# Branch products 2 and 1 of a hybrid decoder layer in seven block products instead of eight

## The chip, the cores and the metric

One core of one Trainium2 chip runs the whole kernel. The metric is the device time of one execution in microseconds (us), the median of three runs. TensorE is called PE, VectorE DVE, ScalarE ACT, GpSimd POOL and SyncE SP; SP issues most loads.

## The reference

All is float32. 576 tokens (512 of a prompt, 64 of eight samples) go through one layer; the two groups are stacked.

```python
xn = rmsnorm(x); proj = xn @ w_in                      # 1024 -> 13440 columns
y_conv = b_gate * conv3(c_gate * h) * silu(g_conv)     # branch 0
y_rwkv = rwkv7(p_shift, ...) * silu(g_rwkv)            # branch 1
y_mem  = attention(q_mem, mem_k, mem_v) * silu(g_mem)  # branch 2
merged = (sigmoid(m_conv) * (y_conv @ w_branch[0])
        + sigmoid(m_rwkv) * (y_rwkv @ w_branch[1])
        + sigmoid(m_mem)  * (y_mem  @ w_branch[2]))    # w_branch[i]: 1024 x 1024
y = rmsnorm(x + merged @ w_out)
```

Also returned are the memory keys and values and the new states.

## The kernel before

**Products.** Activations lie transposed, 128 features by 576 tokens, eight such tiles `k` for 1024 features. Each float32 operand is split into a high part (rounded to float32r) and a low part (the rest), and a product takes three matmuls: high by high, high by low, low by high. `mm` makes one output tile of 128 features: 8 tiles `k` x 3 terms x 2 halves of 288 tokens = 48 matmuls of 288 columns. Its weights are two loads of 128x512 (`wload`): ACT writes the high part `wh`, POOL subtracts for the low part `wl`; both have three buffers.

**The order of the work.** The order of PE's instructions is the order of the Python code. On the other engines a scheduler sets the order of the instructions when the kernel is built, and each engine then runs its list strictly in that order. The last stages run in this order:

1. `drive(gate(WGM, qt))`: eight products with `w_in`; each gives silu(g_mem) and is multiplied into one tile of `qt` (the attention's output).
2. `drive(branch(2, *split(qt)))`: `split` makes the parts `yh`, `yl`. For each output tile `j` there is the gate (a product with `w_in`, or a load if it was made early, in idle slots of the RWKV stage) and the product with `w_br`. DVE multiplies the gate `th` (tile `ev`) by the product in PSUM, POOL adds it to `acc`.
3. `drive(gate(WGR, ow))`: the same as 1 for the RWKV output (tiles `ts4`, `ts4b`).
4. `drive(branch(1, ...))`, where POOL's sum goes on to ACT (`mgh`, the high part) and DVE (`mgl`, the low part). `wout(0)` loads and splits half of `w_out` beside it.
5. The product with `w_out`, the residual and the last norm (L1284).

Seven gates were made early, those of branch 1 for `j` 0 to 6; the other nine are made in stages 2 and 4. PSUM tile `m` (`pm`) has two buffers of two banks. One line of a helper stands for many places: L93 is every `tensor_tensor`, L96 every `scalar_tensor_tensor`, L99 every activation, L245 the matmul in `mm`.

## Time and profile before

| what | us |
|---|---|
| median of 3 runs (1234.75 to 1237.21) | 1235.94 |
| the profiled execution | 1235.45 |
| its span in the trace | 1233.6 |
| PE busy in the span | 1186.9 |
| DVE busy in the span | 587.0 |
| ACT busy in the span | 524.9 |
| POOL busy in the span | 573.8 |

Busy times are unions over the whole span; 1.85 us of the profiled execution lie outside the span. A busy PE means that matmuls follow each other without a gap; it does not say how fast one is.

### The profile page before, as it was taken

The page shows a single profiled execution, that of the slowest core. Times are in us where ns is not written, and L with a number is a line of the kernel's source. Part 1 is how long each engine was busy: PE and PEld are TensorE (multiplying, and loading weights), DVE is VectorE, ACT ScalarE, POOL GpSimd, SP SyncE. Part 2 cuts the span into 40 slices and gives each one's busy share as a digit, 9 for nine tenths or more (in the row PEclk, how much of TensorE's full clock was granted, in tenths as well). Part 3 has the DMA queues.
Part 4 walks back from the last instruction along what each step waited for, and adds up shares of the span by engine and source line. Part 5 has one row for each costly group of instructions (what it writes and reads, how often), then busy time and mean ns, then how long its engine had stood idle before and what let it go on. Part 6 is the DMA issues. An engine that isn't in the chain of part 4 may idle for free. (4 is left out here: it accounts for less than half of the span.)

```text
span 1233.6 us, 25594 instructions
## 1 busy us (share of the span) xinstructions
PE 1186.9 (96%) x10158; PEld 1100.8 (89%) x10158; DVE 587.0 (48%) x1514; ACT 524.9 (43%) x1120; POOL 573.8 (47%) x521
## 2 busy tenths in 40 slices
PE   7999979999899999999989999999999999999997
PEld 7798979989798988988879898889899999999976
DVE  7856866468675686647673315213113100134233
ACT  6563446435463544546344435333233222233222
POOL 4535532555535465454543545333334454446642
PEclk9999989999999999999999999999999999999999
DMA  8642222132321322222322225653632222225522
GB/s 290 213 126 72 70 72 63 59 91 58 91 65 53 89 68 84 90 86 70 110 80 74 69 71 171 195 181 123 208 97 87 80 84 86 78 86 161 161 105 78
DMA packets 93056, 129.39 MB, mean 105 GB/s; under 512 B 36988, under 2 KB 41320, under 8 KB 92936
## 3 DMA queue, kind: packets, MB, share of 16 engines
q1 hardware_dynamic: 55888, 110.20, 28.3%
q10 hardware_dynamic: 37048, 17.56, 5.4%
q8 instruction: 80, 1.31, 0.5%
q14 instruction: 40, 0.33, 0.1%
HBM read 115.96 MB, written 11.47 MB: 103 GB/s over the span
## 5 line engine op out<-in xcount | busy, mean ns | idle before, releaser
L93 POOL TENSOR_TENSOR wl<-w,wh 128x512 fp32r<-128x512 f32 x274 | 366.5, 1340 | 490.0 <-ACT wh L99 451.4
L245 PE MATMUL m<-xh,wh 128*128 128x288 f32 x1680 | 370.4, 302 | 0.5 <-ACT vst L99 0.5
L245 PE MATMUL m<-xl,wh 128*128 128x288 f32 x1680 | 369.4, 301 | 0.0
L245 PE MATMUL m<-xh,wl 128*128 128x288 f32 x1680 | 365.2, 299 | 0.0
L99 ACT ACTIVATE wh<-w 128x512 fp32r<-128x512 f32 x290 | 180.5, 627 | 294.2 <-PE m L245 169.1
L245 PEld LDWEIGHTS m<-xh,wh 128*128 128x128 f32 x1680 | 268.8, 189 | 8.6 <-issue 3.7
L245 PEld LDWEIGHTS m<-xl,wh 128*128 128x128 f32 x1680 | 269.2, 189 | 6.4 <-issue 2.9
L245 PEld LDWEIGHTS m<-xh,wl 128*128 128x128 f32 x1680 | 269.4, 189 | 3.0 <-issue 2.1
L96 DVE SCALAR_TENSOR_TENSOR ev<-ev,m 128x576 f32<-128x576 f32 x32 | 24.2, 755 | 168.4 <-PE m L245 110.3
L245 PE MATMUL m<-yh,wh 128*128 128x288 f32 x384 | 82.9, 297 | 0.0
L245 PE MATMUL m<-yh,wl 128*128 128x288 f32 x384 | 82.8, 297 | 0.0
L245 PE MATMUL m<-yl,wh 128*128 128x288 f32 x384 | 82.8, 297 | 0.0
L245 PEld LDWEIGHTS m<-yh,wl 128*128 128x128 f32 x384 | 61.7, 188 | 2.1 <-issue 2.1
L245 PEld LDWEIGHTS m<-yl,wh 128*128 128x128 f32 x384 | 61.7, 188 | 2.1 <-issue 2.1
L245 PEld LDWEIGHTS m<-yh,wh 128*128 128x128 f32 x384 | 61.7, 189 | 2.1 <-issue 2.1
L93 DVE TENSOR_TENSOR c<-c,tmp 108x84 f32<-108x84 f32 (+23 forms) x248 | 56.6, 228 | 5.4
L93 DVE TENSOR_TENSOR tmp<-c,nin 108x84 f32<-108x84 f32 (+23 forms) x248 | 54.8, 221 | 6.7 <-issue 1.2
L96 DVE SCALAR_TENSOR_TENSOR sb<-o,pcl,sb 64x64 f32<-64x64 f32 x112 | 31.6, 282 | 52.1 <-PE o L887 46.0
L99 ACT ACTIVATE osb<-o 64x128 f32<-64x128 f32 x72 | 19.7, 274 | 52.3 <-DVE sb L96 30.5
L93 DVE TENSOR_TENSOR vu<-o,vu 64x128 f32<-64x128 f32 x56 | 15.9, 284 | 46.6 <-PE o L869 45.6
L99 ACT ACTIVATE E<-m,par 128x32 f32<-128x32 f32 (+1 forms) x75 | 27.2, 418 | 22.2 <-PE m L245 14.1
L99 ACT ACTIVATE sb<-sb,pcl 128x128 f32<-128x128 f32 x56 | 22.5, 401 | 29.4 <-DVE sb L96 18.8
(441 smaller groups left out, 1796.2 us busy)
## 6 DMA issues: line engine op xcount, KB each, us to landing
w<-w_in_in SPq DMA_DIRECT2D x210, 256.0 KB
w<-w_br_in SPq DMA_DIRECT2D x48, 256.0 KB
kb<-kc_in SPq DMA_DIRECT2D x16, 512.0 KB
kb<-vc_in SPq DMA_DIRECT2D x16, 512.0 KB
w<-w_mk_in SPq DMA_DIRECT2D x16, 256.0 KB
w<-w_mv_in SPq DMA_DIRECT2D x16, 256.0 KB
w<-w_o_in SPq DMA_DIRECT2D x16, 256.0 KB
nin<-scr ACTq DMA_DIRECT2D x24, 144.0 KB
```

Of the source, the lines that this page charges most:

```text
L93: e.tensor_tensor(out=out, in0=a, in1=b, op=op)
L96: V.scalar_tensor_tensor(out=out, in0=a, scalar=s, in1=b, op0=op0, op1=op1)
L99: S.activation(out, in_, f, **k)
L245: TE.matmul(ps[:, hf, :n], a[:, f], b[:, k, hf * n:hf * n + n], start=(k == 0 and i == 0), stop=(k == 7 and i == 2))
```

## The change

Stages 2 and 4 are rewritten. Two output tiles and the two halves of the tokens make a 2x2 block problem: the weights of a pair of output tiles are the blocks a11, a12, a21, a22 (128x512 each, four tiles `k`), and the activations of `k` and `k+4` in two token halves the others. `group` makes the pair from seven block products of 12 matmuls each, in the order B11, T1, B21, T2, B22, T3, T4, in place of 2 x 48 matmuls. The sums of activations (T1 to T4) are made once per branch in `Parts.pair`, on DVE, beside the gate stage, which visits `j` in the order 0, 4, 1, 5, 2, 6, 3, 7. The four sums of weights per pair are made on DVE (tiles `a`), and all seven weight operands are split by ACT and DVE; POOL makes none of these any more. Partial results are copied out of PSUM by ACT and added by DVE (`r0`, tile `eR`, and `r1`). Gates that were not made early are now made ahead of stage 1 and kept in DRAM; early ones are first those of branch 2. `wout(0)` now goes to the tiles `s1` and `s2`, which hold the parts of xn until the last product with `w_in` has ended.

```diff
-    EARLY = [(i, j) for i in (1, 2) for j in range(8)]
+    EARLY = [(i, j) for i in (2, 1) for j in range(8)]
...
+    class Parts:
...
+        def pair(self, ys, k):
+            a, b = ys[k], ys[k + 4]
+
+            def two(x, h, l):
+                act(h, x)
+                tt(V, l, x, h.bitcast(F32), ALU.subtract)
+
+            t3 = sp.tile([128, HT], F32, name="t3")
+            tt(V, t3, b[:, H1], a[:, H1], ALU.subtract)
+            tt(V, a[:, H1], a[:, H1], a[:, H0], ALU.subtract)
+            two(a, self.h[:, k, :], self.l[:, k, :])
+            two(b, self.h[:, k + 4, :], self.l[:, k + 4, :])
+            tt(V, b[:, H1], b[:, H1], a[:, H1], ALU.subtract)
+            tt(V, b[:, H0], b[:, H0], b[:, H1], ALU.subtract)
+            two(t3, self.t3[0][:, k, :], self.t3[1][:, k, :])
+            h, l = self.t42[k // 2]
+            two(b, h[:, k % 2, :], l[:, k % 2, :])
...
+    def group(raws, P, following):
...
+        def hl(w):
+            h = wp.tile([128, 512], F32R, name="wh", bufs=3)
+            l = wp.tile([128, 512], F32R, name="wl", bufs=3)
+            act(h, w)
+            tt(V, l, w, h.bitcast(F32), ALU.subtract)
+            return h, l
...
+        def prod(bank, w, n, start, stop):
+            for k in range(4):
+                f = slice(k * 128, k * 128 + 128)
+                for i, (wi, lo) in enumerate(((0, 0), (0, 1), (1, 0))):
+                    TE.matmul(bank, w[wi][:, f], P.op(n, k, lo), start=(start and k == 0 and i == 0),
+                              stop=(stop and k == 3 and i == 2), skip_group_check=True)
...
+        w = hl(a11)
+        tt(V, s1w, a21, a22, ALU.add)
+        yield from prod(a, w, "B11", True, False)
+        act(r0[:, H0], a)
+        w = hl(s1w)
+        tt(V, a21, a11, a21, ALU.subtract)
+        tt(V, s1w, s1w, a11, ALU.subtract)
+        more()
+        yield from prod(e, w, "T1", True, False)
+        act(r1[:, H1], e)
+        w = hl(a12)
+        tt(V, a12, a12, s1w, ALU.subtract)
+        yield from prod(b, w, "B21", True, True)
+        w = hl(s1w)
+        more()
+        yield from prod(a, w, "T2", False, False)
+        act(r0[:, H1], a)
+        w = hl(a12)
+        more()
+        yield from prod(e, w, "B22", False, True)
+        yield from prod(a, hl(a21), "T3", False, True)
+        act(r1[:, H0], a)
+        tt(V, r0[:, H0], b, r0[:, H0], ALU.add)
+        tt(V, r1[:, H1], r1[:, H0], r1[:, H1], ALU.add)
+        yield from prod(c, hl(a22), "T4", True, True)
+        tt(V, r0[:, H1], e, r0[:, H1], ALU.add)
+        tt(V, r1[:, H0], c, r1[:, H0], ALU.add)
...
+    def branch_w(i, P, mgh=None):
...
+            for j, th, r in zip((2 * g, 2 * g + 1), ths, (r0, r1)):
+                stt(th, th, 1.0, r, ALU.add, ALU.mult)
+                ac = acc[j]
+                if mgh is None:
+                    tt(G, ac, ac, th, ALU.add)
+                else:
+                    tt(G, th, ac, th, ALU.add)
+                    act(mgh[j], th, scale=0.5)
...
+                    stt(mgl[j], th, 0.5, mgh[j].bitcast(F32), ALU.mult, ALU.subtract)
...
-    prep_lane.q.append(wout(0, 27))
-    drive(branch(1, *parts, merged=(mgh, mgl)))
+    prep_lane.q.append(wout(0, (168 - 16) // 8 - 1))
+    drive(branch_w(1, P, mgh))
```

DVE's list in branch 2 held one instruction per output tile (`ev` is the gate, `m` the product); here are the first five of its eight, behind the last tile `eF` of stage 1:

```order
L96 SCALAR_TENSOR_TENSOR eF_9646<-ev_11794,eF_9646 128x576
L93 TENSOR_TENSOR yl_11799<-eF_9646,yh_11798 128x576
L96 SCALAR_TENSOR_TENSOR ev_11877<-ev_11877,m_11891 128x576
L96 SCALAR_TENSOR_TENSOR ev_12003<-ev_12003,m_12017 128x576
L96 SCALAR_TENSOR_TENSOR ev_12129<-ev_12129,m_12143 128x576
L96 SCALAR_TENSOR_TENSOR ev_12255<-ev_12255,m_12269 128x576
L96 SCALAR_TENSOR_TENSOR ev_12381<-ev_12381,m_12395 128x576
```

In the changed kernel DVE's list from the end of branch 2's second pair to the start of its third reads as follows. `a_12612`, `a_12614`, `a_12643` are a11, the weight sum and a12 of the third pair, `wl_12783` the low weights of its T1, `wl_12804` of its B21, `wl_12821` of its T2; `eR_12617` and `r1_12618` are the results of the second pair:

```order
L93 TENSOR_TENSOR wl_12783<-a_12614,wh_12782 128x512
L93 TENSOR_TENSOR eR_12617<-m_12615,eR_12617 128x288
L93 TENSOR_TENSOR r1_12618<-r1_12618 128x288
L93 TENSOR_TENSOR eR_12617<-m_12616,eR_12617 128x288
L93 TENSOR_TENSOR r1_12618<-m_12616,r1_12618 128x288
L96 SCALAR_TENSOR_TENSOR ev_12608<-ev_12608,eR_12617 128x576
L96 SCALAR_TENSOR_TENSOR ev_12610<-ev_12610,r1_12618 128x576
L93 TENSOR_TENSOR a_12614<-a_12614,a_12612 128x512
L93 TENSOR_TENSOR wl_12804<-a_12643,wh_12803 128x512
L93 TENSOR_TENSOR a_12643<-a_12643,a_12614 128x512
L93 TENSOR_TENSOR wl_12821<-a_12614,wh_12820 128x512
```

The low weights of the third pair's B21 thus stand behind the whole end of the second pair, and those of its T1 ahead of it.

In branch 1 DVE's list at the same place, between its second and its third pair, holds two more instructions, the low parts `mgl`; each reads what POOL's sum and then ACT (`eA`, `eB`) have written. `wl_14010` belongs to B21, `wl_14027` to T2:

```order
L96 SCALAR_TENSOR_TENSOR ev_13796<-ev_13796,eR_13805 128x576
L96 SCALAR_TENSOR_TENSOR ev_13798<-ev_13798,r1_13806 128x576
L93 TENSOR_TENSOR a_13802<-a_13802,a_13800 128x512
L93 TENSOR_TENSOR wl_14010<-a_13831,wh_14009 128x512
L96 SCALAR_TENSOR_TENSOR mgl_13948<-ev_13796,eA_13616 128x576
L96 SCALAR_TENSOR_TENSOR mgl_13953<-ev_13798,eB_13617 128x576
L93 TENSOR_TENSOR a_13831<-a_13831,a_13802 128x512
L93 TENSOR_TENSOR wl_14027<-a_13802,wh_14026 128x512
```

The low weights of T2 now stand behind both `mgl`.

Where stage 3 passes into branch 1, DVE's list before was, for the last two tiles, `ts4` and `ts4b`:

```order
L96 SCALAR_TENSOR_TENSOR ev_13275<-ev_13275,m_13226 128x576
L96 SCALAR_TENSOR_TENSOR ts4_816<-ev_13275,ts4_816 128x576
L93 TENSOR_TENSOR yl_13357<-ts4_816,yh_13356 128x576
L93 TENSOR_TENSOR wos4_13395<-w_13397,wos3_13391 128x512
L96 SCALAR_TENSOR_TENSOR ev_13340<-ev_13340,m_13291 128x576
L96 SCALAR_TENSOR_TENSOR ts4b_8054<-ev_13340,ts4b_8054 128x576
L93 TENSOR_TENSOR yl_13357<-ts4b_8054,yh_13356 128x576
```

It is now this, where `wos2` is the low part of `w_out` and the last row the last low part that B11 reads:

```order
L96 SCALAR_TENSOR_TENSOR ev_13597<-ev_13597,m_13548 128x576
L93 TENSOR_TENSOR wos2_13650<-w_13651,wos1_13649 128x512
L96 SCALAR_TENSOR_TENSOR ts4b_8054<-ev_13597,ts4b_8054 128x576
L93 TENSOR_TENSOR a_13625<-a_13625,a_13624 128x512
L93 TENSOR_TENSOR t3_13601<-ts4b_8054,ts4_816 128x288
L93 TENSOR_TENSOR yl_13035<-ts4b_8054,yh_13034 128x576
L93 TENSOR_TENSOR ts4_816<-ts4_816 128x288
L93 TENSOR_TENSOR t3l_13041<-t3_13601,t3h_13040 128x288
L93 TENSOR_TENSOR ts4b_8054<-ts4b_8054,ts4_816 128x288
L93 TENSOR_TENSOR wos2_13650<-w_13774,wos1_13649 128x512
L93 TENSOR_TENSOR yl_13035<-ts4_816,yh_13034 128x576
```

The last tile's three instructions have become eleven, two of them for `w_out`; before, one for `w_out` stood ahead of them. The same place ahead of branch 2 has no `wos2`.

## Rows read from the trace of the kernel before

**Rows 1.** The page: the span, and each engine's busy time.
```profile
span 1233.6 us, 25594 instructions
PE 1186.9 (96%) x10158; PEld 1100.8 (89%) x10158; DVE 587.0 (48%) x1514; ACT 524.9 (43%) x1120; POOL 573.8 (47%) x521
```
**Rows 2.** Stages 1 to 4: stretch, length, busy PE, PEld, DVE, ACT, POOL; clock; DMA.
```profile
910.00:961.20 51.20, 51.20 (x387) 51.20 (x386) 16.64 (x22) 17.91 (x31) 21.04 (x16) 1.00 0.25 81
961.20:1063.60 102.40, 102.40 (x771) 102.40 (x770) 7.55 (x10) 25.61 (x43) 51.09 (x39) 1.00 0.27 83
1063.60:1114.80 51.20, 51.20 (x387) 51.20 (x386) 18.31 (x23) 18.53 (x32) 22.44 (x17) 1.00 0.27 82
1114.80:1172.40 57.60, 57.60 (x434) 57.60 (x433) 16.77 (x20) 19.64 (x33) 37.34 (x27) 1.00 0.55 170
```
**Rows 3.** Timeline, end of a stage 3 tile: start, length, engine, operation.
```profile
1102.37 0.63 ACT L99 ACTIVATE ev<-m 128x576 f32<-128x576 f32 x1
1103.03 0.76 DVE L96 SCALAR_TENSOR_TENSOR ev<-ev,m 128x576 f32<-128x576 f32 x1 [3.34 <-ACT ev L99]
1103.82 0.76 DVE L96 SCALAR_TENSOR_TENSOR ts<-ev,ts 128x576 f32<-128x576 f32 x1
```
**Rows 4.** Timeline of DVE: instructions of 288 columns back to back.
```profile
56.30 0.50 DVE L96 SCALAR_TENSOR_TENSOR xn<-tr,par,o 128x288 f32<-128x288 f32 x1
56.73 0.50 DVE L96 SCALAR_TENSOR_TENSOR xn<-tr,par,c 128x288 f32<-128x288 f32 x1
57.15 0.50 DVE L96 SCALAR_TENSOR_TENSOR xn<-tr,par,o 128x288 f32<-128x288 f32 x1
```
**Rows 5.** Timeline of DVE and POOL around three subtractions.
```profile
1112.30 1.34 POOL L93 TENSOR_TENSOR wl<-w,wh 128x512 fp32r<-128x512 f32 x1 [2.06 <-ACT wh L99]
1112.53 1.66 DVE L93 TENSOR_TENSOR wos<-w,wos 128x512 fp32r<-128x512 f32 x1
...
1124.56 0.69 DVE L93 TENSOR_TENSOR wos<-w,wos3c 128x512 fp32r<-128x512 f32 x1 [2.56 <-ACT wos3c L99]
...
1130.95 1.30 POOL L93 TENSOR_TENSOR wos<-w,wos3c 128x512 fp32r<-128x512 f32 x1
1131.62 1.24 DVE L96 SCALAR_TENSOR_TENSOR mgl<-ev,ek 128x576 fp32r<-128x576 f32 x1 [3.23 <-ACT ek L99]
1132.24 1.77 POOL L93 TENSOR_TENSOR wl<-w,wh 128x512 fp32r<-128x512 f32 x1
```
**Rows 6.** Windows (columns as in Rows 2) around two falls of the clock.
```profile
23.90:27.30 3.40, 1.62 (x12) 1.45 (x12) 3.40 (x9) 2.03 (x5) 0.49 (x1) 1.00 0.93 316
27.30:30.70 3.40, 3.40 (x19) 3.40 (x18) 3.30 (x3) 2.28 (x5) 3.30 (x2) 0.50 0.98 335
...
163.80:167.30 3.50, 0.45 (x4) 0.22 (x2) 0.30 (x1) 1.71 (x5) 0.26 (x1) 0.99 0.67 166
167.30:174.00 6.70, 4.28 (x76) 3.94 (x76) 5.43 (x27) 3.23 (x10) 3.55 (x4) 0.50 0.26 82
```
**Rows 7.** Timeline: PE's wait in the first of these stretches.
```profile
24.52 0.71 PE L189 MATMUL c<-dg,ones 128*128 128x128 f32 x4 [2.21 <-DVE dg L179]
```
**Rows 8.** Timeline: a load of 256 KB, and ACT that waited for it.
```profile
1107.26 0.33 SPq L1254 DMA_DIRECT2D w<-w_o_in  x1
...
1109.85 0.63 ACT L99 ACTIVATE wos<-w 128x512 fp32r<-128x512 f32 x1 [0.46 <-DMA w<-w_o_in]
```
**Rows 9.** Timeline of PE: the first product of branch 1.
```profile
1114.64 0.43 PE L245 MATMUL m<-yh,wh 128*128 128x288 f32 x2
```
**Rows 10.** Timeline: an output tile of branch 1 behind its product.
```profile
1122.99 1.43 POOL L93 TENSOR_TENSOR ev<-acc,ev 128x576 f32<-128x576 f32 x1
1124.45 0.69 ACT L99 ACTIVATE er<-ev 128x576 fp32r<-128x576 f32 x1
1125.17 0.76 DVE L96 SCALAR_TENSOR_TENSOR mgl<-ev,er 128x576 fp32r<-128x576 f32 x1
```
**Rows 11.** Timeline: PE's weight load behind the last output tile.
```profile
1177.52 0.19 PEld L1284 LDWEIGHTS m<-wos3b,mgl 128*128 128x128 f32 x1 [0.31 <-DVE mgl L96]
```

More of the change, by code (lines that the diff above doesn't have):

```diff
@@ L192, in inv_rms @@
         out += [rs, bc]
-    lw = [cst.tile([128, 1024], F32R, name="lw%d" % i) for i in range(2)]
+    lw = [cst.tile([128, 1024], F32R, name="lw%d" % i, tag="lw%d" % i) for i in range(2)]
     up, dn = slice(0, 64), slice(64, 128)
@@ L1003, in hybrid_step @@
     late = ctx.enter_context(tc.tile_pool(name="late", bufs=1, reuse_waits="tile"))
-    acc = late.tile([128, 8, T], F32, name="acc")
+    acc = [late.tile([128, T], F32, name="acc", tag="acc%d" % j) for j in range(8)]
     def split(ys):
@@ L1024, in branch @@
             if first:
-                stt(v3(acc[:, j, :]), v3(th), 1.0, m3(ps), ALU.add, ALU.mult)
+                stt(v3(acc[j]), v3(th), 1.0, m3(ps), ALU.add, ALU.mult)
                 continue
@@ L1028, in branch @@
             if merged is None:
-                tt(G, acc[:, j, :], acc[:, j, :], th, ALU.add)
+                tt(G, acc[j], acc[j], th, ALU.add)
             else:
                 mgh, mgl = merged
-                tt(G, th, acc[:, j, :], th, ALU.add)
+                tt(G, th, acc[j], th, ALU.add)
                 act(mgh[j], th, scale=0.5)
@@ L1219, in hybrid_step, with gate @@
         drive(first())
-    def gate(w, ys):
-        for j in range(8):
+    def gate(w, ys, P):
+        for j in PAIRS:
             ps = yield from mm(w_in[w + j])
@@ L1227, in gate, with __init__, op @@
             stt(ys[j], th, 0.5, ys[j], ALU.mult, ALU.mult)
-    drive(gate(WGM, qt))
-    drive(branch(2, *split(qt)))
+            if j > 3:
+                P.pair(ys, j - 4)
+    sp = ctx.enter_context(tc.tile_pool(name="sp", bufs=1, reuse_waits="tile"))
+    fs_ = sp.tile([128, 5, 5], F32, name="fs_")
+    H0, H1 = slice(0, HT), slice(HT, T)
+    class Parts:
+        def __init__(self):
+            self.h = late.tile([128, 8, T], F32R, name="yh", tag="yh")
+            self.l = late.tile([128, 8, T], F32R, name="yl", tag="yl")
+            self.t42 = []
+            for i in range(2):
+                a, b = (keep.tile([128, 2, T], F32R, name="t42", tag=t) for t in SLOTS[2 * i:2 * i + 2])
+                self.t42.append((a, b))
+            self.t3 = [sp.tile([128, 4, HT], F32R, name="t3" + n) for n in "hl"]
+        def pair(self, ys, k):
[13 more added lines that the diff above has]
+            two(b, h[:, k % 2, :], l[:, k % 2, :])
+        def op(self, n, k, lo):
+            y = self.l if lo else self.h
+            if n == "B11":
+                return y[:, k, H0]
+            if n == "T1":
+                return y[:, k, H1]
+            if n == "B21":
+                return y[:, k + 4, H0]
+            if n == "B22":
+                return y[:, k + 4, H1]
+            if n == "T3":
+                return self.t3[lo][:, k, :]
+            return self.t42[k // 2][lo][:, k % 2, H0 if n == "T4" else H1]
@@ new lines, in branch_w @@
+    def branch_w(i, P, mgh=None):
+        raws = list(load_group(w_br[8 * i], w_br[8 * i + 1]))
+        for g in range(4):
+            ths = []
+            for j in (2 * g, 2 * g + 1):
+                th = etile("v", bufs=2)
+                DMA.dma_start(out=th, in_=gates[i, j])
+                ths.append(th)
+            j = 8 * i + 2 * g + 2
+            r0, r1, raws = yield from group(raws, P, load_group(w_br[j], w_br[j + 1]) if g < 3 else None)
+            for j, th, r in zip((2 * g, 2 * g + 1), ths, (r0, r1)):
[6 more added lines that the diff above has]
+                    act(mgh[j], th, scale=0.5)
+                    mgl.append(late.tile([128, T], F32R, name="mgl", tag="acc%d" % j))
+                    stt(mgl[j], th, 0.5, mgh[j].bitcast(F32), ALU.mult, ALU.subtract)
@@ new lines, in other_gates @@
+    def other_gates():
+        for i, j in EARLY:
+            if (i, j) not in gates:
+                ps = yield from mm(w_in[WM[i] + j])
+                t = etile("v", bufs=2)
+                act(v3(t), m3(ps), AF.Tanh, scale=0.5)
+                gates[i, j] = drp.tile([128, T], F32, name="gate%d%d" % (i, j), bufs=1)
+                S.dma_start(out=gates[i, j], in_=t)
+    PAIRS = (0, 4, 1, 5, 2, 6, 3, 7)
+    drive(other_gates())
+    P = Parts()
+    drive(gate(WGM, qt, P))
+    drive(branch_w(2, P))
@@ L1231, in hybrid_step @@
     ow = orw
-    drive(gate(WGR, ow))
-    fin = ctx.enter_context(tc.tile_pool(name="fin", bufs=1, reuse_waits="tile"))
-    mgl = fin.tile([128, 8, T], F32R, name="mgl")
+    P = Parts()
+    drive(gate(WGR, ow, P))
+    mgl = []
     mgh = [etile(t, F32R) for t in QT]
-    parts = split(ow)
     wo = []
@@ L1247, in wout @@
         if n == 0:
-            h, l = place(keep, *((t, 2) for t in SLOTS)), place(keep, ("s4", 7), ("s4b", 1))
+            h, l = place(keep, ("s1", 8)), place(keep, ("s2", 8))
         else:
```

45 lines of the change are left out of this document (36 added, 9 removed).

## The prediction, made before the changed kernel was run

> **What bounds the kernel now.** I read the page first: PE is busy for 1186.9 of 1233.6 us, every other engine for about half [rows 1]. Then the windows of the stages that the change touches: in stages 1 to 4, 262.4 us long, PE is busy for the whole of each window, at a granted clock of 1.00 [rows 2]. So PE is the bound here, and work taken from it pays as long as nobody else makes it wait. DVE is the engine to watch: it is nearly idle here (7.55 of 102.40 us in stage 2) and receives almost all that is added.
>
> **What is taken away.** Stage 2 before is sixteen products of 48 matmuls in 102.40 us [rows 2], so a product takes 6.40 us and a matmul of 288 columns 0.1333. A branch drops from 384 matmuls to 4 pairs x 84 = 336. Two branches save 96 x 0.1333 = **12.8 us**. A pair takes PE 11.2 us instead of 12.8, a block product 1.6. The nine late gates are only moved.
>
> **What is added on DVE.** DVE now has 17 instructions per pair: 7 low parts and 4 weight sums of 512 columns, 4 sums of 288 and 2 of 576. Their prices: a subtraction of 512 takes 0.69 undisturbed [rows 5], instructions of 576 take 0.76 and a dependent one starts 0.79 later [rows 3], those of 288 follow each other at 0.42 [rows 4]. That is 11 x 0.69 + 4 x 0.42 + 0.79 + 0.76 = 10.8 us per pair against PE's 11.2: DVE alone would just keep up. What matters is where it stands in line, and what holds it.
>
> *The chain between two pairs.* The low weights of T1 can only be made when T3 of the pair before has ended and left one of the three buffers. Behind them, in DVE's fixed list, come the four sums, the two gate products, a weight sum, and only then the low weights of B21. From the end of T3: ACT's high part 0.63 [rows 8], low part 0.69, sums 4 x 0.42 = 1.7, gate products 0.79 + 0.76, weight sum 0.69, low part of B21 0.69; in all 5.95. PE has meanwhile T4, B11, T1 and two matmuls of B21, 5.07. It stalls for 0.9.
>
> *POOL holds DVE.* As the gate products end, POOL adds two tiles to `acc`, 1.43 each [rows 10]. A subtraction on DVE took 0.69 alone and 1.66 when it came 0.23 after a POOL subtraction had begun; an `mgl` (0.76 alone [rows 10]) ended 0.6 after POOL did, and POOL's next one took 1.77 instead of 1.30 [rows 5]. Instructions of the two engines with both inputs in SBUF thus take turns. From 1.66 - 0.69 + 0.23, a POOL instruction costs DVE 1.2 if it stands just ahead. Both additions fall in the chain: + 2.4, and a steady stall of branch 2 is **3.3 us** (three times). From below the price is 0, if DVE's next instruction always goes first; I take 1.2 because the rows show turns.
>
> The Trainium skill ("SBUF — State Buffer", section "Who interferes with whom") says that a Vector instruction with two SBUF inputs and a GpSimd instruction that reads SBUF share a port, and that whichever starts first blocks the other for its whole length. By that rule each addition would cost its full 1.43, and the sum below would be about 3 us higher. The trace agrees on the blocking; its 1.66 is a little less than the rule's 1.34 - 0.23 + 0.69 = 1.80.
>
> *Branch 1, steady.* Behind the low part of B21 stand two `mgl` (0.76 each, POOL and ACT being done by then), a weight sum and the low part of T2: 2 x 0.76 + 2 x 0.69 = 2.9. PE covers 12 matmuls, 1.6, so a second stall of 1.3 follows the first: **4.6 us** per pair (three times).
>
> *Entering branch 2.* The last tile of stage 1 ends, and B11 needs the last `yl`. In DVE's order: ACT's tanh 0.7 [rows 3], gate 0.79, a weight sum 0.69, product 0.76, two sums 0.84, `yl` 0.76, low part of T3 0.42, `yl` 0.76: 5.7. ACT's parts fit in between. PE covers 10 matmuls, 1.3: stall **4.4**. Before, a gate's product with `w_in` (6.40) stood there.
>
> *Entering branch 1.* The same, plus two `wos2` on DVE (2 x 0.69) and two on POOL (2 x 1.2), all of which had to wait for `s1` and `s2` until the last product with `w_in` ended: 9.5 - 1.3 = **8.2**. Before, the first product of branch 1 followed without a wait [rows 9], since the last `yl` was needed 5.6 us into it.
>
> *Leaving branch 1.* The last two outputs end together rather than 6.4 us apart. Before, `mgl` was 0.31 late [rows 11]. One more gate product (0.76) and a second POOL addition partly under it make it about **1.0** later.
>
> *The clock.* After a wait of 2.21 us [rows 7] in a stretch in which PE was busy 1.62 of 3.40, the granted clock was 0.50 (1.2 of 2.4 GHz) for the next 3.4 us; after one in which it was busy 0.45 of 3.50, for 6.7 us [rows 6]. The eight stalls above last 3.3 us and more, so I expect the lower level after most of them. A stretch of 3.4 us at half speed costs 1.7 if PE works all through it and nothing if it lies inside the stall or under the second one: 0 to 13.6 for eight; I take 1.0 each, **8 us**.
>
> *Edits costed at nothing.* The pairs' sums in stages 1 and 3 add 5 x 0.42 + 0.76 = 2.9 us of DVE per two tiles, under PE's 12.8; DVE was busy there for 18.31 of 51.20 [rows 2], and over half of its time stays free to absorb turns with POOL. If that cover went, a tile would pay what is over. ACT has seven splits (4.4) and four copies (about 0.4 each, estimated from its 0.63 for 576 columns) per pair, 6 to 8 of 11.2. Loads: a weight block lands 2.6 us after its issue (1107.26 to 1109.85 [rows 8]); SP asks for a22 when the low part of B22 is made and it is first read some 2.5 us later, a tie that DVE's wait for T3 covers; were it 1 us late, up to 1 us per pair would be added. The residual's load is moved in SP's queue ahead of two of them, in branch 1's first pair alone.
>
> *The sum,* against the profiled execution of 1235.45, which stands 0.5 below the median. Stalls: 4.4 + 3 x 3.3 + 8.2 + 3 x 4.6 = 36.3. 1235.45 - 12.8 + 36.3 + 1.0 + 8 = **1268 us**.
>
> **The rivals.**
>
> *The clock stays up:* 1260. For it: no row shows a single wait of 3.3 us between long dense stretches, only a longer one and two shorter ones close together.
>
> *POOL does not hold DVE* (DVE's list is dense, so its next instruction might go first every time, and POOL wait). Stalls then: 4.4 + 3 x 0.9 + 5.8 in the entries and branch 2. In branch 1 an `mgl` still waits for POOL and ACT: two additions 2.9, ACT 0.69, `mgl` 0.76, sum and low part 1.4, so 5.7 from the gate product to T2's low weights, of which PE covers 3.8 beyond the first stall: 1.9 + 0.9 = 2.8, three times. In all 21.3; clock up: 1235.45 - 12.8 + 21.3 + 1 = 1245. Against it are the three rows of turns [rows 5].
>
> *Faster: DVE stays ahead of PE.* Independent instructions of DVE overlap in part: those of 288 last 0.50 but start every 0.42 [rows 4]. If the whole chain between two pairs ran that way, and POOL's additions fell into gaps, it would be shorter than PE's 5.07; the steady stalls vanish in both branches, which is the point from which it decides. With the two entries at 4.4 and 5.8 that is 1234, still no change; it is faster by over 0.2% from 2 us of the entries covered, and 1224 with all of them. Against it: 5.95 is already near the sum of lone instructions, and any POOL addition breaks it.
>
> *Worse:* both the full 13.6 for the clock and late loads of a22 in the six later pairs, 1280.
>
> **How the numbers follow.** The likeliest is the sum, 1268, with the clock's price anywhere from 5 to 13.6 (about 1265 to 1274): 0.47. Clock up: 0.20. POOL not holding DVE: 0.13. Worse: 0.08. DVE ahead of PE: 0.07. The remaining 0.05 is a cancellation of stalls and saving. 0.2% (2.5 us) is about what a measurement of this kernel can tell from no change. Faster 0.07, same 0.05, slower 0.88. The range is 1244 to 1280: from POOL not holding DVE to the upper bound of clock and loads.
>
> **What would show it.** Right: 96 matmuls fewer; a window of branch 2 with PE waiting in each pair inside B21, on DVE's `wl`; in branch 1 a second wait inside T2; one wait of some 4 us at the start of branch 2 and twice that ahead of branch 1, both ended by `yl`; DVE instructions at 1.2 to 1.9 where POOL's `acc` runs; a granted clock below 1 in these windows. Wrong: PE busy throughout (DVE stays ahead); waits ended by ACT or by a load (then I mispriced another engine); `wl` at 0.69 all along (no turns); more or longer waits in stages 1 and 3, where I have none.

## The result: 1269 us, slower by 2.7%

| kernel | median, us | runs (lowest to highest) | ratio to before, 95% interval |
|---|---|---|---|
| before | 1235.80 | 4 (1234.75 to 1237.21) | |
| changed | 1269.28 | 4 (1266.57 to 1273.41) | 1.027 (1.0245 to 1.0294) |

The forecast was 1268 us, slower. The profiled execution of the changed kernel is the slowest of its four runs: 1273.41 us, with a span of 1271.3. The page of the changed kernel, its span and each engine's busy time, answers to [rows 1]:

```profile
span 1271.3 us, 25673 instructions
PE 1191.5 (94%) x10062; PEld 1098.9 (86%) x10062; DVE 703.2 (55%) x1682; ACT 557.4 (44%) x1192; POOL 540.4 (43%) x489
```

PE has the 96 matmuls fewer that the change promised, and is busy for 4.6 us *longer*: some of its matmuls ran at half the clock. Where that is, and where PE stood still, the windows say. These are cut at the first matmul of each of branch 2's four pairs, then of branch 1's four, then of the product with w_out (columns as in [rows 2]):

```profile
1020.75:1039.16 18.41, 14.18 (x87) 13.39 (x85) 12.62 (x22) 8.63 (x17) 0.00 (x0) 0.81 0.28 89
1039.16:1054.88 15.72, 13.21 (x84) 12.74 (x85) 12.41 (x18) 5.68 (x12) 3.69 (x2) 0.89 0.33 105
1054.88:1070.60 15.72, 13.21 (x85) 12.74 (x85) 12.41 (x18) 5.73 (x12) 3.69 (x2) 0.89 0.34 106
1070.60:1084.48 13.88, 11.52 (x84) 11.25 (x85) 11.26 (x16) 5.53 (x11) 5.93 (x4) 1.00 0.39 118
1135.73:1158.06 22.33, 14.65 (x87) 13.86 (x85) 17.05 (x26) 13.01 (x25) 4.46 (x4) 0.77 0.70 227
1158.06:1174.59 16.53, 13.27 (x85) 12.57 (x85) 14.71 (x20) 7.00 (x14) 4.70 (x3) 0.90 0.35 116
1174.59:1190.60 16.01, 13.32 (x84) 12.50 (x84) 13.55 (x20) 6.86 (x14) 3.62 (x2) 0.89 0.22 70
1190.60:1205.94 15.34, 11.92 (x85) 11.22 (x85) 13.03 (x18) 7.12 (x14) 4.91 (x3) 1.00 0.18 57
```

A pair is 84 matmuls, 11.2 us if nothing holds PE. No pair comes near it: the first of each branch takes 18.41 and 22.33, the others 13.9 to 16.5. Stage 2 is 63.73 us long and stage 4 70.21, together 133.94; with the nine gates that were moved out (9 x 6.40) that is 191.5 against 160.0 before. Stages 1 and 3 remain dense (stage 3 takes 51.25 for 51.20).

The waits of PE in these stages, from its timeline (start, length, engine; in brackets the idle time and what ended it): the entry of branch 2, one steady pair of it, the entry of branch 1, its last pair, and the start of the product with w_out:

```profile
1025.79 0.61 PE L1324 MATMUL m<-yh,wh 128*128 128x288 f32 x1 [3.70 <-ACT yh L99]
1026.79 0.61 PE L1324 MATMUL m<-yl,wh 128*128 128x288 f32 x1 [0.39 <-DVE yl L93]
...
1060.96 0.40 PE L1324 MATMUL m<-yh,wl 128*128 128x288 f32 x1 [2.36 <-DVE wl L93]
...
1142.85 0.61 PE L1324 MATMUL m<-yh,wh 128*128 128x288 f32 x1 [5.77 <-ACT yh L99]
1145.22 0.61 PE L1324 MATMUL m<-yl,wh 128*128 128x288 f32 x1 [1.76 <-DVE yl L93]
...
1196.67 0.40 PE L1324 MATMUL m<-yh,wl 128*128 128x288 f32 x1 [2.36 <-DVE wl L93]
1199.21 0.40 PE L1324 MATMUL m<-t,wl 128*128 128x288 f32 x1 [0.70 <-DVE wl L93]
...
1205.94 0.74 PE L1450 MATMUL m<-wos,er 128*128 128x512 f32 x2 [0.36 <-DVE eR L93]
1211.46 0.73 PE L1450 MATMUL m<-wos,eE 128*128 128x512 f32 x2 [1.11 <-ACT eE L99]
1213.18 0.50 PE L1450 MATMUL m<-wos,mgl 128*128 128x512 f32 x1 [0.99 <-DVE mgl L96]
1214.95 0.50 PE L1450 MATMUL m<-wos,mgl 128*128 128x512 f32 x1 [0.80 <-DVE mgl L96]
```

A wait of this kind on `wl` stands in every steady pair of both branches (2.36 or 2.37 in five of the six, 2.83 in branch 1's second pair), always at the third matmul of B21, the first that reads B21's low weights. What DVE did ahead of the one at 1060.96, from its timeline, with POOL's only row there at the end:

```profile
1053.76 0.69 DVE L93 TENSOR_TENSOR wl<-a,wh 128x512 fp32r<-128x512 f32 x1 [0.62 <-ACT wh L99]
...
1057.17 1.92 DVE L93 TENSOR_TENSOR a<-a 128x512 f32<-128x512 f32 x1
1059.02 1.88 DVE L93 TENSOR_TENSOR wl<-a,wh 128x512 fp32r<-128x512 f32 x1
...
1056.67 3.69 POOL L93 TENSOR_TENSOR acc<-acc,ev 128x576 f32<-128x576 f32 x2 [12.03 <-DVE ev L96]
```

DVE has no gap from the low part of T1 (1053.76) to that of B21 (ends 1060.90); PE goes on 0.06 later. In between it made the four sums, the two gate products, the weight sum and this low part. The last two, made while POOL's two additions run, take 1.92 and 1.88 instead of 0.69.

### The profile page after: what moved, and what is told of

It is laid out like the page before. It is cut to its first block, busy times and chain, and to the rows that moved or that the text cites. A ratio compares the mean times of both kernels' runs of the same rounds, so it can differ in the third digit from the quotient of the medians.

```text
span 1271.3 us, 25673 instructions
## 1 busy us (share of the span) xinstructions
PE 1191.5 (94%) x10062; PEld 1098.9 (86%) x10062; DVE 703.2 (55%) x1682; ACT 557.4 (44%) x1192; POOL 540.4 (43%) x489
## 5 line engine op out<-in xcount | busy, mean ns | idle before, releaser
L93 POOL TENSOR_TENSOR wl<-w,wh 128x512 fp32r<-128x512 f32 x242 | 325.8, 1349 | 453.7 <-ACT wh L99 418.7
L99 ACT ACTIVATE wh<-w 128x512 fp32r<-128x512 f32 x258 | 160.3, 627 | 240.9 <-PE m L245 156.6
L93 DVE TENSOR_TENSOR wl<-a,wh 128x512 fp32r<-128x512 f32 x56 | 45.5, 817 | 23.8 <-ACT wh L99 23.6
L99 ACT ACTIVATE wh<-a 128x512 fp32r<-128x512 f32 x56 | 35.1, 631 | 53.5 <-PE m L1324 30.5
L1324 PE MATMUL m<-yh,wl 128*128 128x288 f32 x128 | 42.0, 328 | 14.6 <-DVE wl L93 14.6
L1324 PE MATMUL m<-yh,wh 128*128 128x288 f32 x128 | 42.2, 330 | 10.7 <-ACT yh L99 9.5
L1324 PE MATMUL m<-yl,wh 128*128 128x288 f32 x128 | 41.4, 323 | 2.1 <-DVE yl L93 2.1
L1324 PEld LDWEIGHTS m<-yh,wl 128*128 128x128 f32 x128 | 27.4, 214 | 16.0 <-DVE wl L93 16.0
L93 DVE TENSOR_TENSOR a<-a 128x512 f32<-128x512 f32 x32 | 29.4, 919 | 18.3 <-PE m L245 17.4
L1324 PEld LDWEIGHTS m<-yh,wh 128*128 128x128 f32 x128 | 27.3, 213 | 12.8 <-ACT yh L99 9.9
```

Source lines behind the costliest of these rows:

```text
L93: e.tensor_tensor(out=out, in0=a, in1=b, op=op)
L99: S.activation(out, in_, f, **k)
L1324: TE.matmul(bank, w[wi][:, f], P.op(n, k, lo), start=(start and k == 0 and i == 0), stop=(stop and k == 3 and i == 2), skip_group_check=True)
```

## The experiments

The theory: PE waits at the seams between pairs and stages, since DVE's list holds everything that ends one pair ahead of the low weights that the next one needs, POOL lengthens that list, and nothing stands there for PE to do; the clock falls on top. The rivals are that POOL costs DVE nothing, that the clock alone is the loss, and that the loss comes from elsewhere (loads, the moved gates). The kernel before ran again beside each group of experiments; its medians were 1234.9 to 1235.1.

### POOL's additions left out: no_acc_add

```diff
-                if mgh is None:
-                    tt(G, ac, ac, th, ALU.add)
-                else:
+                if mgh is not None:
```

> The changed kernel without POOL's eight additions to acc in branch 2 (the output then lacks branch 2's share). Theory: POOL's two additions, 3.7 us of POOL per pair, hold DVE for 1.2 us each where PE waits for it. Then the weight sum and the low part behind them fall from 1.92 and 1.88 to about 0.7 us, the wait of 2.36 us in each steady pair of branch 2 shrinks to 0.5 or less, the clock does not fall there, the steady pair goes from 15.7 to about 11.7 us and stage 2 from 63.8 to about 54; about 1259 us. Rival: DVE's own list is what is late, and it would be slow without POOL too: these instructions stay near 1.9, the wait stays above 2, stage 2 at 62 to 64, 1267 to 1271 us.

Measured: 1264.09 us, ratio 1.0242 (1.0225 to 1.0259). DVE's weight sum and low part of B21 in the third pair, and the window of the second:

```profile
1051.73 0.68 DVE L93 TENSOR_TENSOR a<-a 128x512 f32<-128x512 f32 x1
1052.34 0.68 DVE L93 TENSOR_TENSOR wl<-a,wh 128x512 fp32r<-128x512 f32 x1
```
```profile
1037.70:1049.44 11.74, 11.59 (x84) 11.20 (x85) 9.96 (x18) 5.69 (x12) 0.00 (x0) 1.00 0.45 141
```

1.92 and 1.88 have become 0.68 each, the pair 11.74 with the clock at 1.00, and stage 2 is 53.01 us long instead of 63.73: there it is as the theory said, and the rival falls. The median is 5 us above the theory's 1259, and only 5.2 below that of the changed kernel. The profile here ends 11.6 us earlier, but it is the fastest of its four runs, and the changed kernel's the slowest.

### Idle matmuls in the waits: fill_waits

Ahead of B21 stand none in branch 2's first pair and 14 in the other seven pairs, ahead of each branch 26:

```diff
+    def fill(P, n):
+        z = psd.tile([128, 512], F32, name="s")
+        for _ in range(n):
+            TE.matmul(z[:, 0:HT], P.h[:, 0, 0:128], P.h[:, 0, 0:HT], start=True, stop=True)
...
+        fill(P, fills.pop(0))
         yield from prod(b, w, "B21", True, True)
...
+        fill(P, 26)
```

> The changed kernel with idle matmuls (288 columns, result unused) put where PE waits: 26 ahead of each branch and 14 ahead of B21 in seven of the eight pairs; 2 x 26 + 7 x 14 = 150 x 0.133 = 20 us of work for nothing. Theory: they lie inside the waits, and the clock no longer falls in stages 2 and 4. There 102 matmuls ran at half level, 0.133 us lost on each, 13.6 in all, so the time falls by 8 to 13 us, to 1256 to 1261, with the same arrival of DVE's low weights in each pair. Rival 1: the lost clock was hidden under the same waits, and DVE's chain sets the pair whatever the clock does: the waits grow, 1267 to 1272. Rival 2: the added matmuls cost their time: up to 1289.

Measured: 1271.43 us, 1.0308 (1.0284 to 1.0331). Nothing was gained, which is the time of rival 1; but the windows don't bear out its reason, and they say why this settles less than it should. They show branch 2's second, third and fourth pair:

```profile
1033.05:1047.30 14.25, 13.69 (x99) 13.08 (x99) 12.34 (x18) 5.57 (x12) 3.71 (x2) 1.00 0.34 104
1047.30:1061.94 14.64, 13.77 (x99) 13.09 (x98) 12.04 (x18) 5.72 (x12) 4.93 (x2) 1.00 0.36 115
1061.94:1079.85 17.91, 14.75 (x100) 14.28 (x99) 12.71 (x16) 5.65 (x12) 7.60 (x4) 0.93 0.33 110
```

In the first two the clock stays up and the pair is 1.1 to 1.5 us shorter, with 1.9 us of idle work in it. The fourth pair is 4.0 us *longer* than in the changed kernel. The added instructions had moved the scheduler's order: two weight sums of branch 1, stages ahead of their use, now stood in DVE's list in front of the low part of T4, and waited for their load. DVE's timeline, and PE's wait for the low part behind them:

```profile
1073.67 2.97 DVE L93 TENSOR_TENSOR a<-a 128x512 f32<-128x512 f32 x2 [3.26 <-DMA a<-w_br_in]
```
```profile
1077.29 0.60 PE L1331 MATMUL m<-t,wl 128*128 128x288 f32 x1 [2.98 <-DVE wl L93]
```

Branch 1's first pair has no wait at B21 in the changed kernel; it got 14 idle matmuls all the same, and is 1.7 us longer (24.07 for 22.33). So the total is inconclusive; it remains that a fall of the clock costs a steady pair of branch 2 1.1 to 1.5 us, and that idle matmuls, as they were put here, gained nothing. The theory's 0.133 us lost on each matmul at half level was too much: in the changed kernel's second pair they follow each other at 0.24 us there (1045.65, 1045.89, 1046.13) instead of 0.133, so 0.107 is lost.

### Five buffers for the weight parts: ring_of_five

```diff
+    hn = [0]
...
+            hn[0] += 1
+            if hn[0] % 5 < 3:
+                h = wp.tile([128, 512], F32R, name="wh", bufs=3)
+                l = wp.tile([128, 512], F32R, name="wl", bufs=3)
+            else:
+                x = cst.tile([128, 1024], F32R, name="lx", tag="lw%d" % (hn[0] % 5 - 3))
+                h, l = x[:, 0:512], x[:, 512:1024]
```

> The changed kernel with five buffers instead of three for the weight parts wh and wl of the pairs. Theory: the wait comes from the order that three buffers force (the low weights of T1 wait for T3 of the pair before, those of B21 stand behind the whole end of the pair). With five, DVE's list has the low weights of T1 and B21 ahead of the four sums, the wait in B21 goes, and what is left is DVE's own time, 10.8 us a pair plus 2.4 for POOL's turns, 13.2 against 15.7 now, in six pairs: about 15 us less, 1254; the waits move to T2 or later and stay under 2 us. Rival 1: DVE keeps ahead of PE, pairs of 11.3 us, about 1243. Rival 2: the raw blocks or their loads are late instead, no gain, 1265 to 1272.

Measured: 1256.16 us, 1.0179 (1.0163 to 1.0194). The second and third pair of branch 2:

```profile
1035.53:1047.17 11.64, 11.52 (x84) 11.28 (x85) 11.57 (x17) 5.31 (x11) 3.72 (x2) 1.00 0.46 137
1047.17:1059.83 12.66, 11.43 (x87) 11.11 (x85) 12.59 (x19) 6.44 (x12) 3.73 (x2) 1.00 0.45 136
```

No wait on `wl` is left in either branch; POOL still adds to `acc` here. It was the order in DVE's list, as three buffers force it, that turned DVE's time into PE's waits on `wl`. DVE is busy for nearly the whole of both pairs, so they are as short as DVE allows, and shorter than the 13.2 of the theory. Where DVE is still late, PE now waits at the start of a pair, on the sum in `eR`: 1.24 us ahead of branch 2's fourth pair, 2.11 ahead of branch 1's third. The total is near the theory's all the same, since part of the gain is lost later: from the product with w_out on the program takes 69.51 us instead of 65.4.

### Gates at the entries: gate_at_entries

```diff
-    def other_gates():
-        for i, j in EARLY:
-            if (i, j) not in gates:
+    def other_gates(n):
+        for i, j in [g for g in EARLY if g not in gates][:n]:
...
-    drive(other_gates())
+    drive(other_gates(9 - 2))
     P = Parts()
     drive(gate(WGM, qt, P))
+    drive(other_gates(1))
     drive(branch_w(2, P))
...
     drive(gate(WGR, ow, P))
+    drive(other_gates(1))
```

> The changed kernel with one of the nine late gates (a product with w_in, 6.4 us of PE) made between stage 1 and branch 2 and one between stage 3 and branch 1, instead of ahead of stage 1. No work is added or taken away. Theory: the two entries (waits of 3.70 + 0.39 and 5.77 + 1.76 us, and 46 matmuls at half clock behind them, 6.1 us) are DVE's and ACT's sums with nothing for PE to do beside them; with 6.4 us of cover both waits shrink to under 1.5 us and the clock stays up: 11 to 17 us less, 1252 to 1258. Rival: the sums are only pushed later, since the gate's own tanh and splits stand in the same lists, and the first pair waits instead: 1264 to 1270.

Measured: 1261.36 us, 1.0218 (1.0201 to 1.0236), between the two. Windows of branch 2's second and third pair and of branch 1's second:

```profile
1022.76:1038.45 15.69, 13.18 (x84) 12.71 (x84) 12.38 (x18) 5.67 (x12) 3.68 (x2) 0.89 0.36 105
1038.45:1052.65 14.20, 11.69 (x84) 11.21 (x84) 12.41 (x18) 5.74 (x12) 3.69 (x2) 1.00 0.41 116
...
1137.68:1159.71 22.03, 15.90 (x84) 14.36 (x84) 18.48 (x23) 9.88 (x19) 8.04 (x5) 0.77 0.49 162
```

Branch 2's first pair went from 18.41 to 11.46 (1011.30 to 1022.76): there the theory holds. In branch 1 the waits at the entry are gone too, but the gain is not: the first pair went from 22.33 to 14.92, 3.15 of it a wait at its end, and the second from 16.53 to 22.03. The rival had the lateness come from the gate's own tanh and splits. The trace shows something else first, a load. ACT's queue, SP's queue and DVE there:

```profile
1124.04 0.33 ACTq L1389 DMA_DIRECT2D gate<-ev  x1
1131.53 0.33 SPq L1366 DMA_DIRECT2D ev<-gate  x1
1135.84 1.42 DVE L93 TENSOR_TENSOR a<-a 128x512 f32<-128x512 f32 x2 [3.22 <-DMA a<-w_br_in]
```

The new gate is stored from a tile `ev`; SP's next load into a tile `ev` went out 7.5 us after that store, and the raw blocks of the next pair stand right behind it (1131.90), so DVE waited 3.22 us for one. The splits of w_out, which wait for the last product with `w_in`, then stand in the second pair. The two upper rows price the clock: two pairs with the same matmuls and the same DVE time, one at 0.89 and one at 1.00, differ by 1.49 us.

### One branch at a time: branch2_only, branch1_only

Branch 2 alone in seven products (stage 3, branch 1 and the end as before), and branch 1 alone:

```diff
-    drive(gate(WGR, ow, P))
+    drive(gate(WGR, ow, None))
...
+    parts = split(ow)
...
-    drive(branch_w(1, P, mgh))
+    drive(branch(1, *parts, merged=(mgh, mgl)))
```
```diff
-    drive(gate(WGM, qt, P))
-    drive(branch_w(2, P))
+    drive(gate(WGM, qt, None))
+    drive(branch(2, *split(qt)))
```

> Only branch 2 in seven products; stage 3, branch 1 and the product with w_out as before (the gates of branch 1 are made inside it again). Theory (the losses are local to a branch): stage 2 takes 63.7 us as in the changed kernel, 18.9 over its 44.8 us of matmuls; branch 1 keeps PE busy; so 1235 - 6.4 + 18.9 = about 1248. Rival: the branches disturb each other (the moved gates, the moved w_out), and this is 1241 or less, or above 1255.

> Only branch 1 in seven products, branch 2 as before with its gates inside. Theory (losses are local): stage 4 takes 70.2 us, 25.4 over its 44.8 us of matmuls, and the product with w_out begins with 4 us of waits: 1235 - 6.4 + 25.4 + 4.2 = about 1258, and this excess and that of branch 2 alone add up to the changed kernel's 34. Rival: branch 1 would not lose more than branch 2 (1248), so that part of its loss came from the stages ahead of it.

Measured: 1246.39 us, 1.0089 (1.0073 to 1.0105), and 1261.93, 1.0214 (1.0194 to 1.0234). That is 11.3 and 26.8 us over the kernel before, 38 together; the changed kernel is 33.5 over it, so together they are 4.6 us more than it. Both losses are there without the other branch, and stages 2 and 4 are as long as in the changed kernel within a fall or two of the clock (61.38 for 63.73, 69.34 for 70.21). Branch 1 costs 3.9 us more than expected; its end, from the product with w_out on, takes 67.56 us, with a clock of 0.95.

### Gates between the pairs: gates_between, gates_between_k_last

`SHARE` is one gate ahead of each of branch 2's four pairs and of branch 1's first three:

```diff
         for g in range(4):
+            yield from other_gates(SHARE[i][g])
+            if i == 1 and g == 2:
+                prep_lane.q.append(wout(0, (84 - 8) // 8 - 1))
```

The second kernel has this as well, in the product with w_out:

```diff
+        if hf == 0:
+            two = [pm.tile([128, 2, 512], F32, name="m") for _ in range(2)]
+            for ks in (range(6), range(6, 8)):
+                for i in range(2):
+                    part(two[i], i, 128, 0, 512, ks)
```

> The changed kernel with seven of the nine late gates (6.4 us of PE each, little DVE) spread: one ahead of each of branch 2's four pairs and of branch 1's first three, instead of all nine ahead of stage 1; wout(0), which needs the tiles that those gates read, then runs beside branch 1's last two pairs. The same PE work. Theory: the loss is DVE's chain at each seam with nothing for PE beside it; 6.4 us there covers the 2.4 us waits, both entries and the clock falls. Pairs of 11.3 to 11.8 us in branch 2; left are branch 1's last pair (about 4) and the leaving (4): 1235 - 12.8 + 8 = 1226 to 1233, below the kernel before or equal to it. Rival: each gate brings two low parts on POOL, which hold DVE in turn (1.2 us each) inside a pair, and ACT's tanh and splits; the waits come back inside the pairs: 1240 to 1255.

> As gates_between, and the product with w_out makes its first two output tiles side by side: tiles k 0 to 5 of both, then k 6 and 7 of both. The same matmuls. Theory: the waits of 3.3 us at the start of that product are the last pair's results (mgl of k 6 and 7) needed 3.8 us after its first matmul; now they are needed 7.7 us after it, and the waits go: 2.5 to 4 us below gates_between. Rival: the last pair ends so late that w_out's own splits or the results of k 0 to 5 are waited for: within 1 us of gates_between.

Measured: 1244.21 us, 1.0071 (1.0053 to 1.0089), and 1237.55, 1.0023 (1.0013 to 1.0033). Windows of gates_between_k_last: branch 2 (four pairs, three gates between them), branch 1's last two pairs, and the end:

```profile
979.41:1043.38 63.97, 63.97 (x483) 63.82 (x481) 47.08 (x64) 28.90 (x55) 20.99 (x14) 1.00 0.44 142
1140.26:1172.80 32.54, 25.30 (x171) 23.89 (x169) 27.97 (x36) 17.63 (x35) 10.78 (x7) 0.95 0.42 135
1172.80:1234.78 61.98, 55.11 (x264) 44.59 (x264) 23.97 (x36) 15.52 (x34) 21.42 (x21) 0.99 0.19 64
```

With a gate ahead of each pair, branch 2 has no wait: PE is busy for all of 63.97 us, which is 4 x 11.2 + 3 x 6.40 = 64.0. DVE has the same work, and POOL has more. The rival (POOL's low parts bring the waits back) falls for branch 2. Beginning the w_out product with two tiles side by side took its 66.03 us to 61.98; before the change it took 61.4. The median fell by 6.7 us, more than the theory's 2.5 to 4; 4.05 of it is this. But gates_between itself is 11 us above its theory's upper end, in the rival's range, and what was left is in branch 1. The two uncovered pairs of branch 1, with w_out's splits beside them, take 32.54 for 22.4; and PE waits 2.8 us after branch 1's first pair, since DVE, at 1113.28, has waited 4.45 us for raw blocks. SP's queue ahead of that:

```profile
1100.97 8.13 SPq L1369 DMA_DIRECT2D ev<-gate  x2
1109.14 1.39 SPq L1286 DMA_DIRECT2D a<-w_br_in  x3
```

The raw blocks of the next pair stand behind a load into tile `ev`, the second of the two, which went out at 1108.77; I read this as a wait for the gate that was stored from that tile, as in gate_at_entries.

### The rest covered: gates_8 to last_gate_direct

Four steps, each on top of the one before: a gate ahead of branch 1's last pair too, with w_out's first half in two parts (tiles k 0 to 3 into s4 and s4b from the start of the branch, k 4 to 7 into s1 after the last gate); tiles of their own for the gates' tanh; branch 1's additions on DVE; and the last gate used where it was made:

```diff
+    prep_lane.q.append(wout(0, 40, range(4)))
...
-                t = etile("v", bufs=2)
+                t = cst.tile([128, T], F32, name="gt", tag="lw%d" % (j % 2))
...
-                    tt(G, th, ac, th, ALU.add)
+                    tt(V, th, ac, th, ALU.add)
...
-                DMA.dma_start(out=th, in_=gates[i, j])
+                if (i, j) in gates:
+                    DMA.dma_start(out=th, in_=gates[i, j])
+                else:
+                    ps = yield from mm(w_in[WM[i] + j])
+                    act(v3(th), m3(ps), AF.Tanh, scale=0.5)
```

> As gates_between_k_last, with a gate ahead of branch 1's fourth pair too (one gate is left ahead of stage 1), and wout(0) in two parts: tiles k 0 to 3 go to the tiles of the RWKV output, free from the start of branch 1, and only k 4 to 7 wait for the last product with w_in. Theory: branch 1's last two pairs took 16.6 and 15.3 us because they had no cover and all eight splits of w_out beside them; with cover and half the splits spread they take 12 or less: 6 to 8 us below gates_between_k_last, 1229 to 1232, below the kernel before. Rival: the late loads seen in branch 1's first pair (DVE at the head of its list waited 4.45 us for a raw block) come in every pair now, since each pair has a gate ahead of it: 1235 to 1240.

> As gates_8, and the gates made between the pairs write their tanh into tiles of their own, so that the loads of a pair's two gates don't wait for the tile ev to be stored first. Theory: SP's queue stood behind such a load in branch 1's first pair (a load of ev issued 7.8 us after the one before it, and the raw blocks right behind it), which made PE wait 2.8 us; that wait goes in each pair of branch 1: 2 to 6 us below gates_8. Rival: the load was late for the ring of raw blocks, and nothing changes (within 1 us).

> As gates_8_own_tile, and branch 1's eight additions to acc are made on DVE (0.76 us each) instead of on POOL. Theory (an addition on POOL costs DVE 1.2 us where it stands just ahead): DVE gains 0.9 us a pair, and the last pair's results come 1 us earlier: 0 to 3 us below gates_8_own_tile, since most of the chain is covered by now. Rival: with the cover there DVE has more work in the chain ahead of the low weights, and this is 1 to 3 us slower.

> As gates_8_dve_adds, and the gate made ahead of branch 1's last pair, which that pair itself needs, stays in the tile ev instead of going through DRAM. Theory: in gates_8_dve_adds the load of this gate could be issued only 8 us after its store (1153.57 to 1161.56), the loads of w_out stood behind it in SP's queue and were split late, ahead of the last pair's results in ACT's and DVE's lists, and the product with w_out began with a wait of 5.6 us. Without the round trip that wait falls to 1 us or less: about 5 us below gates_8_dve_adds, 1228 to 1231, below the kernel before by 0.3 to 0.5%. Rival: the loads of w_out are late because the tiles of xn come free only with this gate; the wait stays above 3 us, 1232 to 1236.

| kernel | median, us | ratio to before, 95% interval |
|---|---|---|
| gates_8 | 1236.92 | 1.0018 (1.0004 to 1.0033) |
| gates_8_own_tile | 1236.07 | 1.0013 (1.0001 to 1.0026) |
| gates_8_dve_adds | 1234.43 | 0.9992 (0.9979 to 1.0004) |
| last_gate_direct | 1228.28 | 0.9943 (0.9926 to 0.9961) |

The first two missed their theories; gates_8_own_tile came out as its rival said, and the steps of 0.9 and 1.6 us that follow gates_8 are less than the scatter of the runs. Branch 1's last two pairs got shorter in gates_8: 12.3 us and, up to a new wait at its end, 12.6, for 16.6 and 16.0. PE's wait behind its first pair fell from 2.8 to 0.5 in gates_8 and 0.3 in gates_8_own_tile. Most of it was thus gone before the gates had tiles of their own, so my reading of it is not shown; with such tiles the two loads do go out ahead of the store (1088.7 and 1091.8, the store at 1096.6). A new wait took the gain, 3.60 us in gates_8, 4.57 and 5.61 in the next two. In gates_8_dve_adds it is this, at the start of the product with w_out; behind PE's row stand ACT's store of the last gate, SP's queue after it, and the splits of w_out on ACT and DVE:

```profile
1169.66 1.22 PE L1452 MATMUL m<-wos,er 128*128 128x512 f32 x2 [5.61 <-DVE eR L93]
...
1153.57 0.33 ACTq L1392 DMA_DIRECT2D gate<-gt  x1
...
1161.56 0.33 SPq L1369 DMA_DIRECT2D ev<-gate  x1
1161.98 1.33 SPq L1427 DMA_DIRECT2D w<-w_o_in  x3
...
1165.70 0.63 ACT L99 ACTIVATE wos<-w 128x512 fp32r<-128x512 f32 x1 [5.58 <-DMA w<-w_o_in]
1168.26 0.69 DVE L93 TENSOR_TENSOR woyl<-w,woyh 128x512 fp32r<-128x512 f32 x1 [7.71 <-ACT woyh L99]
```

The load of this gate could only be issued 8.0 us after its store, w_out's loads stood behind it, and their splits stood in ACT's and DVE's lists ahead of the last pair's results. With that round trip gone the wait is gone, and the kernel is 6.2 us faster than gates_8_dve_adds and 6.9 faster than the kernel before. The windows of last_gate_direct, branch 2 and branch 1:

```profile
971.38:1037.96 66.58, 64.26 (x483) 63.72 (x481) 50.60 (x64) 28.90 (x55) 23.23 (x14) 1.00 0.43 129
1095.54:1164.16 68.62, 65.21 (x482) 63.84 (x480) 54.11 (x79) 36.07 (x69) 15.32 (x11) 1.00 0.49 158
```

The clock is at 1.00 in both branches. What is left of waits there, 2.3 and 3.4 us of idle PE, was not pursued.

## Why the prediction was right, and where its sizes were off

The measured sizes are those of the changed kernel's profile, which ends 38.0 us after the one before; the medians differ by 33.5.

| term | forecast, us | measured, us | from |
|---|---|---|---|
| matmuls saved | -12.8 | -12.8 | 96 fewer |
| entering branch 2 | 4.4 | 4.1 | 3.70 + 0.39 |
| steady pairs of branch 2 | 9.9 | 9.0 | 3 x (14.20 at clock 1.00 - 11.2) |
| entering branch 1 | 8.2 | 7.5 | 5.77 + 1.76 |
| steady pairs of branch 1 | 13.8 | 11.3 | 3 x (15.34 - 0.36 - 11.2) |
| clock | 8 | 12.1 | the rest of 133.94 - 8 x 11.2, less 0.36 |
| leaving branch 1 | 1.0 | 4.4 | 65.4 against 61.4, and the 0.36 |
| ahead of stage 2 | 0 | 2.1 | the start of stage 2, less the 57.6 of the gates |

**The bound and the saving** were as read: PE was the bound, and a pair that nothing holds takes 11.1 us (each of branch 2 in gates_between_k_last).

**The chain and POOL's turns.** Forecast 3.3 a pair, measured 3.0 at full clock. no_acc_add showed both parts: without POOL's additions 0.5 is left (11.74 - 11.2) where 0.9 was forecast. That the list's order makes it a wait of PE, ring_of_five showed. The two rivals that needed DVE to be fast, POOL not holding it and DVE ahead of PE, are out by the 1.92 and 1.88. A late block a22, which the rival for a still worse result needed, ended no wait of PE in the changed kernel.

**The entries** came 0.3 and 0.7 below the forecast, and for the reason given (branch 2: gate_at_entries). I named `yl` as the last to arrive; the longer part was ended by ACT's `yh`, which stands just ahead of it and reads the same sums. A wait ended by ACT was among my signs of being wrong, but ACT begins this `yh` 0.04 us after the end of DVE's sum in both entries (1025.02, 1142.08), so it is still DVE's list that comes late. That two splits of w_out on each of DVE and POOL make the second entry longer was not tried by itself. The trace has DVE's two in their places, 0.68 us each, and beside POOL's two DVE's product took 1.82 us (1138.26) and a sum 1.52 (1142.37), together 2.1 us more than alone, where I had 2.4.

**Branch 1's second wait** was over-sized: 0.18 and 0.70 us, and none listed in the second pair, where I had 1.3. It is 0.7 where the clock stayed up (also 0.69 in the second pair of branch1_only); where the clock fell, PE comes to T2 later and the wait hides behind that.

**The clock** fell after six of the eight waits, not after the last pair's of either branch, though these were as long (2.37 and 2.36). In branch2_only the second and third pair had the same wait too and stayed at 1.00 (14.19 and 14.18 us). What decides it these runs don't show. Two of the falls at half level, after a steady pair's wait and in the entry of branch 1 (windows; columns as above):

```profile
1045.22:1048.63 3.41, 3.39 (x14) 3.39 (x15) 2.09 (x4) 1.26 (x2) 0.00 (x0) 0.50 0.69 222
...
1140.79:1151.03 10.24, 6.42 (x25) 6.10 (x26) 8.25 (x13) 5.78 (x12) 2.75 (x2) 0.50 0.76 241
```

After the steady waits PE worked all through the stretch, so it costs nearly the 1.7 of the forecast's upper bound: 1.5 by the two pairs of gate_at_entries, and 1.5 by count, 14 matmuls that lose 0.107 each. In branch 1 part of it falls together with the second wait. The entries cost more, over 3 us each by difference (18.41 - 11.2 - 4.1, 22.33 - 11.2 - 7.5), and there the level stayed low for 6.83 and 10.24 us. By count, 21 and 25 matmuls, the clock has 2.2 and 2.7 of that; the rest is PE's start behind each wait (a matmul of 0.61 us in the rows above, where 0.44 is usual at this level and 0.29 at full clock). In all 102 matmuls ran at the low level, 10.9 us of the 12.1. The step that failed is the 1.0 for each stall: I had let the stretches lie half inside the waits.

**Leaving branch 1** is the step that was wrong by most: four waits of 3.26 us together where I had 1.0. DVE's timeline there, behind the last pair's sums:

```profile
1207.57 1.85 DVE L96 SCALAR_TENSOR_TENSOR ev<-ev,r 128x576 f32<-128x576 f32 x1
1209.34 1.91 DVE L93 TENSOR_TENSOR woyl<-w,woyh 128x512 fp32r<-128x512 f32 x1
1211.44 1.69 DVE L96 SCALAR_TENSOR_TENSOR mgl<-ev,eE 128x576 fp32r<-128x576 f32 x1 [0.20 <-ACT eE L99]
1213.26 1.63 DVE L96 SCALAR_TENSOR_TENSOR mgl<-ev,eF 128x576 fp32r<-128x576 f32 x1
```

Four instructions in a row are held by POOL, 0.9 to 1.2 us each, one of them a split of w_out in between (POOL has the two additions and such splits; it is busy 8.94 of the 11.06 us behind 1205.94). I had priced one gate product and part of an addition, and the turns not at all, though I had used them everywhere else. gates_between_k_last took 4.0 us off by letting PE need the last results later.

**Ahead of stage 2** PE is busy for the whole of the 108.95 us in which the nine gates and stage 1 are made (57.6 + 51.2 = 108.8), so nearly all of the 2.1 lies before them, where the code differs in little but which gates are made early. The clock's low level lasted longer early on in this run (6.83 us at 24.64 against 3.41 at 27.31), but PE reaches the same point only 0.8 us later behind it (32.98 for 32.20); the rest stays open. Stage 2 begins between 1016.8 and 1020.8 in the changed kernel's profile and those of the three experiments that leave the stages before it alone.

The misses partly cancel: + 4.1 clock, + 3.4 leaving, - 4.4 the four lines of waits, + 2.1 ahead of stage 2. This profile is 5 us above the sum, and the median of the runs 4.1 below this profile; so the time was hit more closely than its parts, and that much is luck.

## What to carry to other kernels

Work taken from the engine that bounds a kernel pays only where the engines that feed it are ahead at the seams; add up the in-order list of the feeding engine between the last result of one step and the first operand of the next, and compare that with what the bounding engine still has to do meanwhile, not the busy shares. If the list is longer, look for work of the bounding engine that needs none of it and put it into the seam: the nine gates cost 57.6 us wherever they stand, and moving eight of them from one block to the seams, with the small edits that this called for, turned 1269 us into 1228. Then follow each new wait to its queue: the last 6 us were a store and load of one tile through DRAM with unrelated loads behind it, and what reads like the same path held up branch 1 in gate_at_entries.
